# The first layer's output projection beside its last attention head

## The chip, the cores and the metric

The kernel runs on one core of a Trainium2 chip. The metric is device time in microseconds. Its engines have their own instruction queues: TensorE (PE; weight loads stand apart as PEld), VectorE (DVE), ScalarE (ACT), GpSimd (POOL) and SyncE (SP), which only issues transfers here. A profile has the times of one execution.

## The reference, cut to what matters

A two-layer transformer on 1024 image tokens and 256 context tokens, width 1024, in fp32. Layer 0 mixes by differential attention, layer 1 by windowed attention; each is followed by a residual, a norm, and a mixture of 32 experts. What the change touches is the end of layer 0's mixer:

```python
def _diff_attend(q, k, v, lam):
    s = jnp.einsum('bqhmd,bkhmd->bhmqk', q, k).astype(jnp.float32) / math.sqrt(q.shape[-1])
    p = jax.nn.softmax(s, axis=-1)
    a = p[:, :, 0] - lam * p[:, :, 1]
    return jnp.einsum('bhqk,bkhd->bqhd', a.astype(v.dtype), v)
...
    def out_proj(o):
        o = _rmsnorm(o, subln_g) * (1.0 - lam_init)
        return o.reshape(o.shape[0], o.shape[1], -1) @ w_o
    y = out_proj(_sweep_queries(lambda qb: _diff_attend(qb, k_all, v_all, lam), q))
    if not need_ctx:
        return y, None
    qc = qc.reshape(b, -1, DA_HEADS, 2, HEAD_DIM)
    return y, out_proj(_diff_attend(qc, kc, vc, lam))
...
        x = x + g1 * y
        h2 = _modulate(_rmsnorm(x, norm2_g[i]), sh2, sc2).reshape(b * s, d)
```

There are 8 heads of 128 columns, each with two score maps. An image token sees all 1280 keys; a context token only the 256 context keys. The norm in `out_proj` is per head, over 128 columns, with a weight vector of 128 that all heads share.

## The kernel before

Tokens go in ten tiles of 128: 0 to 7 are image, 8 and 9 context. Products of fp32 values run as three matmuls, of a high and a low half on each side (`woh`, `wol`; "hi" is a rounded copy made on ScalarE, "lo" the difference). Outside the experts, a planner sorts each engine's instructions by the priority of their order in the program and by costs of its own, and gives tiles their buffers; a tile waits until the buffer's last reader is done.

`attention0` goes through heads 0 to 7. In head h, for query tile j, it runs a plan, a string of steps written by hand (`PLAN0`, for the last head `PLAN0L`): `S` computes one map's scores into the only score buffer (three PSUM banks), `E` evicts them on VectorE with the row's bound (L590), `X` takes the exponential on ScalarE (L598), `C` combines the two maps (L612 to L615). `T` transposes two key tiles for a pair of query tiles, with copies on ScalarE and VectorE (L543 to L547); `V` multiplies with the values (L556 to L558). `Q` pulls matmuls of the next head's projection (L341), `P` and `K` take its results, `M` advances the modulation vectors (`gen_mods`, on ScalarE and GpSimd), `W` advances a list of weight loads and splits. In head 7 there is no next head: `W` there loads and splits the output projection's weights, `wo_open`, through two raw buffers (L716 on ScalarE, L717 on GpSimd). Each pair's result goes to memory (`o_s`).

Then `oproj` runs the output projection tile by tile, in the order of `PLANO[0]`: `I` loads a tile of `o_s` and of x, `N` norms the heads two tiles ahead (`norm_o`: L771 on ScalarE, L773 and L778 on VectorE, L779 on GpSimd), `A` transposes one tile ahead, `Q` pulls the 48 matmuls of the tile (L805), and for the tile before, `C` adds the residual (L837 to L839), `L` computes the router's logits, `S` and `H` norm (L857), `D` and `E` route. `get_rows` loads four rows of modulation vectors, once for the image tiles and once for the context tiles. `ring_load` prefetches expert weights, seven chunks of 1 MB, two at a step. Layer 1 uses the same function, and there its first three steps run beside the last units of attention.

Of the kernel before, what the change touches and what calls it, by code (L numbers as in the profile page):

```python
# [3 lines left out]

# [37 lines left out]
MODS = (28, 0)  # L42
# [22 lines left out]
PLAN0L = "S0 E0 X0 V P W S1 V T W V V V E1 X1 K C"  # L65
# [29 lines left out]
class Kernel:  # L95
# [8 lines left out]
    def consts(self, es):  # L104
# [27 lines left out]
        self.cos = c.tile([P, NX, 64], F32, name="cos")  # L132
        self.sin = c.tile([P, NX, 64], F32, name="sin")
# [17 lines left out]
        self.gneg = c.tile([P, P], F32, name="gneg")  # L151
# [219 lines left out]


    def attention0(self, es_wo, es_raw):
        nc, tc, A = self.nc, self.tc, self.A
        with ExitStack() as es:
            ea, ep = ExitStack(), ExitStack()
# [3 lines left out]
            ps_t = self.pool(es, "a0t", bufs=2, space=PSUM)  # L380
# [47 lines left out]
            nc.sync.dma_start(self.cos, A["cos"])  # L428
            nc.sync.dma_start(self.sin, A["sin"])
# [5 lines left out]
            nc.vector.tensor_scalar(self.gneg, sg, -(1.0 - LAM0), None, op0=OP.mult)  # L435
# [9 lines left out]
            def new_k(h):  # L445
                K[h] = pk.tile([P, 2, NT * P], F32R, name=f"K{h % 2}")

            def new_v(h):
                V[h] = [pk.tile([P, NT, P], F32R, name=f"V{x}{h % 2}") for x in "hl"]
# [70 lines left out]
            pl = self.pool(es, "a0s", side="right")  # L520
            pS = self.pool(es, "a0S", space=PSUM)
            ps_o = self.pool(es, "a0o", space=PSUM)
            ps_q = self.pool(es, "a0r", bufs=2, space=PSUM)
# [4 lines left out]
            modq = deque([self.gen_mods(blocks[:MODS[0]], pl, ps_t)])  # L528
            self.mods_left = blocks[MODS[0]:]

            trq, mmq = deque(), deque()

            def av(h, j0, a0, a1, ks):
# [5 lines left out]
                def tr(i0):  # L539
# [4 lines left out]
                    at = pl.tile([P, 2, 512], F32R, name="aT", bufs=3)  # L544
# [5 lines left out]
                def mm(i0, at):  # L550
# [8 lines left out]
                    if i0 == n - 2:  # L559
                        st["ot"] = pl.tile([P, 256], F32, name="ot", bufs=2)  # L560
                        nc.scalar.activation(st["ot"], oT, AF.Copy)

                def fin():
# [3 lines left out]
                    ob = pl.tile([P, 2, P], F32, name="ob", bufs=2)  # L567
# [52 lines left out]
            for h in range(8):  # L620
# [13 lines left out]
                for j in range(NT):  # L634
                    n = NT * P if j < NX else 256
                    qk = deque()
                    if nxt:
                        ps = ps_q.tile([P, 512], F32, name="qkv")
                        qk.append(self.gen_qkv_mm(ps, hTl.pop(j), W[h + 1], 0, 384))
                    x = {}  # L640

                    def run(o):
# [23 lines left out]
                        elif o == "W" and parts:  # L666
                            parts.popleft()()

                    for o in (PLAN0 if h < 7 else PLAN0L).split():
                        run(o)  # L670
                    E1 = x["1"][0]
# [9 lines left out]
                    if j % 2:  # L681
# [3 lines left out]
            while modq:  # L685
                pull(modq)
            while trq:
                pull_tr()
            while parts:
                parts.popleft()()  # L690
# [8 lines left out]
    def wo_open(self, l, es, es_raw, bufs=2):  # L699
# [21 lines left out]
    def oproj_open(self, l, es, side, ps_t, ps_y, ytag):  # L721

        nc, tc, A = self.nc, self.tc, self.A
        T = NT if l == 0 else NX
        xsrc = A["xin"] if l == 0 else self.xs[1]
# [33 lines left out]
        def stage_load(t):  # L759
            ot = pl.tile([P, D], F32, name="o_in", bufs=OB[l][0])  # L760
            nc.sync.dma_start(ot, self.os[t * P:(t + 1) * P, :])
            xt = pl.tile([P, D], F32, name="x_in", bufs=OB[l][1])
            self.o["load"] = nc.sync.dma_start(xt, xsrc[t * P:(t + 1) * P, :])
            st[t] = dict(o=ot, x=xt)

        def norm_o(t):
# [3 lines left out]
            sq = pl.tile([P, D], F32, name="sq", bufs=1)  # L770
            nc.scalar.activation(sq, ot, AF.Square)  # L771
# [1024 lines left out]
```

## Time and profile before

| what | value |
|---|---|
| median of 3 runs | 3031.5 us (3025.55 to 3036.97) |
| the profiled execution's own time | 3026.7 us |
| its span, first to last instruction | 3024.9 us |
| mean granted TensorE clock | 0.963 |
| PE, PEld busy | 2798.5, 2365.9 us |
| DVE, ACT, POOL busy | 2366.1, 2100.2, 940.2 us |

Busy times are sums over instructions on an engine; on PE, instructions overlap in a pipeline. The granted clock is a share of 2.4 GHz. The output projection of layer 0 lies between 897 and 1085 us, its last head between 818 and 897.

### The profile page before, as it was taken

The numbers are of one execution on the slowest core, as the hardware profiler recorded it, in microseconds if no ns is written. First come the engines' busy times: TensorE is split into PE (matmuls) and PEld (weight loads), VectorE is DVE, ScalarE is ACT, GpSimd is POOL, SyncE is SP. The second block draws the span as 40 slices with busy tenths as digits, with TensorE's granted clock in tenths as the row PEclk, the third lists the DMA queues.
The fourth block names the chain that finished last, engine by engine and source line by source line (L and its number), as shares of the span: only waits on it lengthen the run. The fifth ranks groups of instructions, "written<-read, shape, count | busy, mean of one in ns | idle before, by whom it ended". The sixth has DMA issues, their size and how long they took to land. (4 is left out here: it accounts for less than half of the span.)

```text
span 3024.9 us, 44265 instructions
## 1 busy us (share of the span) xinstructions
PE 2798.5 (93%) x15262; PEld 2365.9 (78%) x15262; DVE 2366.1 (78%) x4074; ACT 2100.2 (69%) x3725; POOL 940.2 (31%) x857
## 2 busy tenths in 40 slices
PE   7999999999979979999999489998999799999995
PEld 3888888888857768888888478887888688888882
DVE  5778777777778879998999777765666799998996
ACT  5777777777762258888888478876553478888882
POOL 5656665665521111111110344655100111111100
PEclk9999999999989989999999689999999899999997
DMA  7644554444335379999999745434226699999995
GB/s 266 237 160 160 178 177 163 165 162 159 128 104 201 139 276 372 384 379 375 376 374 364 267 163 197 145 141 173 95 100 207 246 365 377 372 369 365 368 384 225
DMA packets 303213, 745.51 MB, mean 246 GB/s; under 512 B 24612, under 2 KB 80520, under 8 KB 287624
## 3 DMA queue, kind: packets, MB, share of 16 engines
q1 hardware_dynamic: 263880, 676.53, 62.2%
q0 software_dynamic: 19584, 41.98, 3.6%
q10 hardware_dynamic: 19520, 24.12, 2.2%
q8 instruction: 122, 2.00, 0.3%
q14 instruction: 107, 0.88, 0.1%
HBM read 680.60 MB, written 91.29 MB: 255 GB/s over the span
## 5 line engine op out<-in xcount | busy, mean ns | idle before, releaser
L1096 DVE TENSOR_TENSOR elo<-wr,ehi 128x1024 fp32r<-128x1024 f32 x768 | 893.5, 1217 | 104.3 <-ACT ehi L1094 104.2
L1094 ACT ACTIVATE ehi<-wr 128x1024 fp32r<-128x1024 f32 x768 | 763.0, 1062 | 3.1 <-DMA wr<-in_wd 1.3
L341 PE MATMUL qkv<-w_hi,hT 128*128 128x384 f32 (+1 forms) x1920 | 546.1, 353 | 14.8 <-ACT hT L312 4.7
L341 PEld LDWEIGHTS qkv<-w_hi,hT 128*128 128x128 f32 x1920 | 355.6, 197 | 31.4 <-issue 14.0
L1123 POOL DMA_INDIRECT y_s<-yb,dI x64 | 65.7, 1026 | 966.5 <-ACT yb L1172 936.9
L341 PE MATMUL qkv<-w_lo,hT 128*128 128x384 f32 (+1 forms) x960 | 336.0, 350 | 0.4 <-POOL w_lo L332 0.4
L1162 PE MATMUL y<-ehi,hidT 128*128 128x512 f32 x1024 | 316.5, 390 | 2.4 <-ACT yb L1172 2.4
L1148 PE MATMUL pg<-ehi,xT 128*128 128x512 f32 x1024 | 291.4, 407 | 3.3 <-ACT ehi L1094 3.3
L1148 PE MATMUL pu<-ehi,xT 128*128 128x512 f32 x1024 | 281.5, 396 | 0.0
L590 DVE TENSOR_SCALAR_CACHE_REDUCE E<-S 128x1280 f32<-128x1280 f32 (+1 forms) x160 | 203.4, 1271 | 61.1 <-PE S L607 59.7
L1162 PEld LDWEIGHTS y<-ehi,hidT 128*128 128x128 f32 x1024 | 191.8, 188 | 43.7 <-ACT yb L1172 3.2
L598 ACT ACTIVATE E<-E,mx 128x1280 f32<-128x1280 f32 (+1 forms) x160 | 191.0, 1194 | 49.6 <-DVE E L590 48.8
L1148 PEld LDWEIGHTS pu<-ehi,xT 128*128 128x128 f32 x1024 | 188.1, 188 | 36.8
L1148 PEld LDWEIGHTS pg<-ehi,xT 128*128 128x128 f32 x1024 | 184.9, 191 | 36.9 <-ACT ehi L1094 4.1
L1162 PE MATMUL y<-elo,hidT 128*128 128x512 f32 x512 | 199.7, 390 | 0.0
L341 PEld LDWEIGHTS qkv<-w_lo,hT 128*128 128x128 f32 x960 | 188.9, 197 | 6.6 <-issue 4.3
L224 ACT ACTIVATE mpr<-mraw,sf 128x256 f32<-128x256 f32 x320 | 145.5, 504 | 28.8 <-POOL macc L227 22.1
L605 PE MATMUL S<-K,Qh 128*128 128x512 f32 (+1 forms) x416 | 152.6, 367 | 13.2 <-DVE E L590 13.1
L1148 PE MATMUL pg<-elo,xT 128*128 128x512 f32 x512 | 160.0, 394 | 0.0
L1148 PE MATMUL pu<-elo,xT 128*128 128x512 f32 x512 | 158.3, 390 | 0.0
L365 POOL TENSOR_TENSOR rd<-rp_a,rp_u 128x256 f32<-128x256 f32 (+1 forms) x96 | 90.7, 945 | 205.4 <-DVE rp_u L360 114.0
L1172 ACT ACTIVATE yb<-y 128x512 f32<-128x512 f32 x126 | 68.5, 595 | 123.7 <-PE y L1162 123.7
(304 smaller groups left out, 6590.0 us busy)
## 6 DMA issues: line engine op xcount, KB each, us to landing
wr<-in_wg SPq DMA_DIRECT2D x128, 1024.0 KB
wr<-in_wu SPq DMA_DIRECT2D x128, 1024.0 KB
wr<-in_wd SPq DMA_DIRECT2D x128, 1024.0 KB
hT<-hTs SPq DMA_DIRECT2D x100, 1024.0 KB
mraw<-in_mod_w SPq DMA_DIRECT2D x80, 512.0 KB
hTs<-hT SPq DMA_DIRECT2D x20, 1024.0 KB
c_y<-y_s SPq DMA_DIRECT2D x28, 512.0 KB
w_raw<-in_a_qkv SPq DMA_DIRECT2D x32, 384.0 KB
```

The source lines that it names most:

```text
L224: nc.scalar.activation(pr[v][:, q], raw[:, q], AF.Copy, scale=self.sf[:, 4 * i + q, v:v + 1])
L341: self.nc.tensor.matmul(ps[:, 0:n], hT[:, a, k, :], W[b][:, k, c0:c0 + n], start=(i == 0), stop=(i == 3 * KC - 1))
L365: nc.gpsimd.tensor_tensor(rd[:, :, 0, :], av, uu, op=OP.add)
L590: nc.vector.tensor_scalar(E[:, 0:n], Sf[:, 0:n], -0.125, None, op0=OP.mult, op1=OP.min, accum_out=mx)
L598: nc.scalar.activation(E[:, 0:n], E[:, 0:n], AF.Exp, bias=mx, scale=-1.0, accum_out=acc)
L605: nc.tensor.matmul(Sf[:, n0:n0 + w], Qh[:, m, j * P:(j + 1) * P], K[h][:, m, o:o + w], start=True, stop=False)
L1094: nc.scalar.activation(hi, raw, AF.Copy)
L1096: nc.vector.tensor_tensor(lo[:, 0:c], raw[:, 0:c], hi[:, 0:c].bitcast(F32), op=OP.subtract)
L1123: nc.gpsimd.indirect_dma_start(out=self.ybs[l], out_offset=bass.IndirectOffsetOnAxis(ap=idx, axis=0), in_=yb, in_offset=None, bounds_check ...
L1148: nc.tensor.matmul(o, xt[:, a, k, :], w[:, q * 512:(q + 1) * 512], start=(k == 0 and a == 0 and w is hi), stop=(k == KC - 1 and w is lo))
L1162: nc.tensor.matmul(y[:, half, :], hT[:, a, k, :], w[:, f], start=(k == 0 and a == 0 and w is hi), stop=(k == 3 and w is lo))
L1172: nc.scalar.activation(yb[:, f], y[:, half, :], AF.Copy)
```

## The change

The projection's steps for the first five tiles are put into the plan of the last head's last five query tiles. For that, the last head takes its tiles in the order 8, 9, 0, ..., 7, and so does the projection. Before the last head, the modulation and the open weighted sums are drained and the pool `a0d` (`pm`) is closed; the eight raw weight tiles are all loaded at its start and split under the second to fourth of its ten tiles. The norm of the heads goes to ScalarE: eight squares with sums and eight scaled copies per tile. The norm's weights, now one column per partition, multiply the rows of the projection's weights at their split; the low half of that split moves from GpSimd to VectorE. Tables for the rotation move to pools of their stages and are loaded again in layer 1. Some buffers move to the pool `pm`, which heads 0 to 6 use.

```diff
-MODS = (28, 0)
+MODS = 28
-PLAN0L = "S0 E0 X0 V P W S1 V T W V V V E1 X1 K C"
+PLAN0L = ("S0 E0 X0 V S1 T W V T E1 X1 W V T V W T V T C",
+          "S0 Q4 E0 X0 T N Q4 T V N S1 Q6 T V N E1 X1 Q4 N T V N Q6 T N V Q8 N T V N Q8 C N Q8 N N")
+ORDER0 = [8, 9] + list(range(8))
+OST0 = 5
...
+    def load_rope(self, pool):
+        self.cos = pool.tile([P, NX, 64], F32, name="cos")
+        self.sin = pool.tile([P, NX, 64], F32, name="sin")
+        self.nc.sync.dma_start(self.cos, self.A["cos"])
+        self.nc.sync.dma_start(self.sin, self.A["sin"])
...
-            nc.vector.tensor_scalar(self.gneg, sg, -(1.0 - LAM0), None, op0=OP.mult)
+            sgT = ps_t.tile([P, 4, P], F32, name="tr")
+            nc.tensor.transpose(sgT[:, 0, :], sg, self.ident)
+            nc.vector.tensor_scalar(self.gneg, sgT[:, 0, 0:1], -(1.0 - LAM0), None, op0=OP.mult)
...
-                K[h] = pk.tile([P, 2, NT * P], F32R, name=f"K{h % 2}")
+                K[h] = (pa, pk)[h % 2].tile([P, 2, NT * P], F32R, name=f"K{h % 2}")
...
-                    at = pl.tile([P, 2, 512], F32R, name="aT", bufs=3)
+                    p = pm if h < 7 and next(nat) % 3 == 2 else pl
+                    at = p.tile([P, 2, 512], F32R, name="aT", bufs=1 if p is pm else 2)
...
-                        st["ot"] = pl.tile([P, 256], F32, name="ot", bufs=2)
+                        st["ot"] = pl.tile([P, 256], F32, name="ot", bufs=1)
...
-                E = pl.tile([P, NT * P], F32, name=f"E{m}", bufs=(4 if m else 2))
+
+                p = pm if m and h < 7 and j % 4 == 3 else pl
+                E = p.tile([P, NT * P], F32, name=f"E{m}", bufs=1 if p is pm else 3 if m else 2)
...
+                    while modq:
+                        pull(modq)
+                    while trq:
+                        pull_tr()
+                    em.close()
                     ea.close()
-                    parts.extend(self.wo_open(0, es_wo, es_raw))
+                    parts.extend(self.wo_open(0, es_wo, es_raw, KC))
+                    for _ in range(KC):
+                        parts.popleft()()
...
-                for j in range(NT):
+                for u, j in enumerate(range(NT) if nxt else ORDER0):
                     n = NT * P if j < NX else 256
+                    ticks = deque()
+                    if not nxt and u == OST0 - 1:
+                        while parts:
+                            parts.popleft()()
+                        es_raw.close()
+                        self.oproj_open(0, es_o, "left", ps_t, ps_q, "qkv")
+                        self.o["start"]()
...
+                    elif u >= OST0:
+                        qk.append(self.o["stage_b"](u - OST0))
+                        ticks.append(self.o["step"](u - OST0, False))
...
+                        elif o == "N":
+                            pull(ticks)
+                        elif o == "W" and parts and (nxt or u):
...
+                    pull(qk, 100)
+                    pull(ticks, 100)
+                    if not nxt and u % 2 == 0:
+                        while trq:
+                            pull_tr()
...
-            nc.scalar.activation(hi[:, k, :], r, AF.Copy)
-            nc.gpsimd.tensor_tensor(lo[:, k, :], r, hi[:, k, :].bitcast(F32), op=OP.subtract)
+            h = hi[:, k, :].bitcast(F32)
+            if l == 0:
+
+                nc.scalar.activation(hi[:, k, :], r, AF.Copy, scale=self.gneg)
+                nc.vector.scalar_tensor_tensor(lo[:, k, :], r, self.gneg, h, op0=OP.mult, op1=OP.subtract)
+            else:
+                nc.scalar.activation(hi[:, k, :], r, AF.Copy)
+                nc.gpsimd.tensor_tensor(lo[:, k, :], r, h, op=OP.subtract)
...
+        tok = (lambda t: ORDER0[t]) if l == 0 else lambda t: t
...
-            sq = pl.tile([P, D], F32, name="sq", bufs=1)
-            nc.scalar.activation(sq, ot, AF.Square)
             w = pl.tile([P, 2, KC], F32, name="ssq", bufs=2)
-            nc.vector.tensor_reduce(w[:, 0, :], sq.rearrange("p (h d) -> p h d", d=P), axis=AX.X, op=OP.add)
-            nc.vector.scalar_tensor_tensor(w[:, 1, :], self.sums[:, t, :], EPS, self.sums[:, t, :],
+            for h in range(KC):
+                sq = pl.tile([P, P], F32, name="sq", bufs=1)
+                nc.scalar.activation(sq, ot[:, h * P:(h + 1) * P], AF.Square, accum_out=w[:, 0, h:h + 1])
+            nc.vector.scalar_tensor_tensor(w[:, 1, :], self.sums[:, tok(t), :], EPS, self.sums[:, tok(t), :],
                                            op0=OP.mult, op1=OP.mult)
             r = self.rsqrt(w[:, 0, :], 1.0 / P, pl, add=w[:, 1, :])
-            ov = ot.rearrange("p (h d) -> p h d", d=P)
-            nc.vector.tensor_tensor(ov, ov, bc(r, P, 2), op=OP.mult)
-            nc.gpsimd.tensor_tensor(ov, ov, bc(self.gneg, KC, 1), op=OP.mult)
+            for h in range(KC):
+                f = slice(h * P, (h + 1) * P)
+                nc.scalar.activation(ot[:, f], ot[:, f], AF.Copy, scale=r[:, h:h + 1])
...
-        if l == 0:
-            ps_t = self.pool(es, f"o{l}t", bufs=2, space=PSUM)
-            ps_y = self.pool(es, f"o{l}y", bufs=2, space=PSUM)
-            es_raw.close()
-            self.oproj_open(l, es, "left", ps_t, ps_y, "y")
...
-            self.o["start"]()
-            t0 = 0
-        else:
-            t0 = 4 * NX + 3 - OSTART
+        t0 = NT - OST0 if l == 0 else 4 * NX + 3 - OSTART
...
             ld = {t: self.combine_load(0, t, pre, 2) for t in order[:3]}
+            self.load_rope(pk)
```

## Rows read from the trace of the kernel before

**Rows 1.** Busy time by stretches of the last head and the projections.

```profile
core 0: us, PE busy (x) PEld busy (x) DVE busy (x) ACT busy (x) POOL busy (x), PEclk, DMA share, GB/s
818.00:861.10 43.10, 31.86 (x147) 24.98 (x147) 30.20 (x45) 28.70 (x45) 20.88 (x8) 0.80 0.33 104
861.10:881.30 20.20, 18.13 (x116) 14.68 (x115) 18.88 (x29) 13.03 (x23) 0.00 (x0) 1.00 0.10 33
881.30:907.40 26.10, 13.84 (x90) 11.30 (x90) 17.26 (x47) 12.94 (x28) 2.34 (x1) 0.79 0.57 186
907.40:1073.00 165.60, 157.63 (x851) 132.00 (x851) 135.29 (x395) 45.52 (x95) 21.48 (x9) 0.98 0.46 162
```

**Rows 2.** Busy time by stretches, layer 1: projection beside attention, then alone.

```profile
2240.00:2275.00 35.00, 35.00 (x218) 29.86 (x217) 24.57 (x68) 23.08 (x45) 0.00 (x0) 1.00 0.26 98
2300.00:2360.00 60.00, 60.00 (x332) 51.13 (x331) 40.50 (x146) 13.72 (x30) 0.00 (x0) 1.00 0.64 224
```

**Rows 3.** Timeline of VectorE, layer 1's projection alone, L857: start, duration.

```profile
2308.83 1.28 DVE L857 SCALAR_TENSOR_TENSOR h<-tmp,rsq,b 128x1024 f32<-128x1024 f32 x1
2323.93 1.28 DVE L857 SCALAR_TENSOR_TENSOR h<-tmp,rsq,b 128x1024 f32<-128x1024 f32 x1
```

**Rows 4.** Groups by line, 897 to 1096: busy, mean ns, idle before.

```profile
L779 POOL TENSOR_TENSOR o_in<-o_in,gneg 128x1024 f32<-128x1024 f32 x10 | 23.8, 2382 | 156.3 <-DVE o_in L778 77.8 <-DVE slot L897 31.4 <-ACT rsq L272 18.3
...
L778 DVE TENSOR_TENSOR o_in<-o_in,rsq 128x1024 f32<-128x1024 f32 x10 | 12.2, 1222 | 0.3
L773 DVE TENSOR_REDUCE ssq<-sq 128x8 f32<-128x1024 f32 x10 | 12.1, 1212 | 3.7 <-ACT sq L771 3.7
...
L870 DVE TENSOR_SCALAR gl<-lgp,m 128x4 f32<-128x4 f32 x10 | 9.3, 934 | 0.0
```

**Rows 5.** Timeline of TensorE, first tiles of the last head.

```profile
818.00 0.39 PE L605 MATMUL S<-K,Qh 128*128 128x512 f32 x1
818.23 0.40 PE L607 MATMUL S<-K,Ql 128*128 128x512 f32 x1
...
821.22 0.39 PE L605 MATMUL S<-K,Qh 128*128 128x256 f32 x1
...
829.98 0.63 PE L607 MATMUL S<-K,Ql 128*128 128x512 f32 x1
830.40 0.63 PE L605 MATMUL S<-K,Qh 128*128 128x512 f32 x1
```

**Rows 6.** Timeline of VectorE, the last key tile of the last head.

```profile
820.73 0.43 DVE L476 TENSOR_TENSOR K<-tr,K 64x256 fp32r<-64x256 f32 x1
```

**Rows 7.** Timeline of VectorE, first and last of the context tiles' four evictions (L590).

```profile
881.31 0.42 DVE L590 TENSOR_SCALAR_CACHE_REDUCE E<-S 128x256 f32<-128x256 f32 x1
...
885.85 0.42 DVE L590 TENSOR_SCALAR_CACHE_REDUCE E<-S 128x256 f32<-128x256 f32 x1
```

**Rows 8.** Groups by line, 818 to 897: the splits of the projection's weights.

```profile
L717 POOL TENSOR_TENSOR wol<-wo_raw,woh 128x1024 fp32r<-128x1024 f32 x8 | 20.9, 2616 | 15.3 <-ACT woh L716 15.3
...
L716 ACT ACTIVATE woh<-wo_raw 128x1024 fp32r<-128x1024 f32 x8 | 8.4, 1054 | 6.3 <-DMA wo_raw<-in_a_wo 6.2
```

**Rows 9.** Timeline of ScalarE, narrow activations at the end of head 6.

```profile
809.21 0.29 ACT L463 ACTIVATE Vh<-qkv 128x128 fp32r<-128x128 f32 x1
...
809.77 0.92 ACT L224 ACTIVATE mraw<-mraw,sf 128x256 f32<-128x256 f32 x2
```

**Rows 10.** Timeline of ScalarE, a table load in layer 1's overlapped part.

```profile
2241.70 0.60 ACT L1532 ACTIVATE aT<-tr 128x512 fp32r<-128x512 f32 x1 [0.42 <-PE tr L1529]
2242.31 1.28 ACT L268 ACT_TABLE_LOAD   x1
2243.61 0.29 ACT L268 ACTIVATE rsq<-ss,eps 128x1 f32<-128x1 f32 x1
```

**Rows 11.** Busy time by stretches, start of layer 1's attention.

```profile
1700.00:1720.00 20.00, 14.45 (x65) 13.37 (x65) 18.72 (x32) 12.19 (x28) 12.68 (x8) 0.59 0.92 325
```

**Rows 12.** Busy time by stretches, in the last head's second tile.

```profile
830.00:835.00 5.00, 3.83 (x12) 2.85 (x11) 2.80 (x3) 4.72 (x6) 3.55 (x2) 0.50 0.44 120
```

More of the change, by code (lines that the diff above doesn't have):

```diff
@@ L3 @@
 from contextlib import ExitStack
+from itertools import count
 import numpy as np
@@ L150, in consts @@
         self.lam = c.tile([P, 1], F32, name="lam")
-        self.gneg = c.tile([P, P], F32, name="gneg")
+        self.gneg = c.tile([P, 1], F32, name="gneg")
         self.dI = c.tile([P, NE], I32, name="dI")
@@ L445, in new_k @@
             def new_k(h):
-                K[h] = pk.tile([P, 2, NT * P], F32R, name=f"K{h % 2}")
+                K[h] = (pa, pk)[h % 2].tile([P, 2, NT * P], F32R, name=f"K{h % 2}")
             def new_v(h):
-                V[h] = [pk.tile([P, NT, P], F32R, name=f"V{x}{h % 2}") for x in "hl"]
+                V[h] = [(pa, pk)[h % 2].tile([P, NT, P], F32R, name=f"V{x}{h % 2}") for x in "hl"]
             new_v(1)
@@ L520, in attention0 @@
             pl = self.pool(es, "a0s", side="right")
+            pm = self.pool(em, "a0d", side="right")
+            ps_q = self.pool(es_o, "a0r", bufs=2, space=PSUM)
             pS = self.pool(es, "a0S", space=PSUM)
             ps_o = self.pool(es, "a0o", space=PSUM)
-            ps_q = self.pool(es, "a0r", bufs=2, space=PSUM)
             S = pS.tile([P, 3, 512], F32, name="S")
@@ L527, in attention0 @@
             blocks = [(0, b) for b in range(8, 24)] + [(1, b) for b in range(24)]
-            modq = deque([self.gen_mods(blocks[:MODS[0]], pl, ps_t)])
-            self.mods_left = blocks[MODS[0]:]
+            modq = deque([self.gen_mods(blocks[:MODS], pm, ps_t)])
+            self.mods_left = blocks[MODS:]
             trq, mmq = deque(), deque()
+            nat = count()
             def av(h, j0, a0, a1, ks):
@@ L566, in fin @@
                         nc.tensor.transpose(pt[:, i, :], st["ot"][:, i * P:(i + 1) * P], self.ident)
-                    ob = pl.tile([P, 2, P], F32, name="ob", bufs=2)
+                    ob = pl.tile([P, 2, P], F32, name="ob", bufs=1)
                     nc.scalar.activation(ob, pt[:, 0:2, :], AF.Copy)
@@ L665, in run @@
                             pull(modq)
-                        elif o == "W" and parts:
+                        elif o == "N":
+                            pull(ticks)
+                        elif o == "W" and parts and (nxt or u):
                             parts.popleft()()
-                    for o in (PLAN0 if h < 7 else PLAN0L).split():
+                    for o in (PLAN0 if nxt else PLAN0L[u >= OST0]).split():
                         run(o)
+                    pull(qk, 100)
[3 more added lines that the diff above has]
+                            pull_tr()
                     E1 = x["1"][0]
@@ L760, in stage_load @@
             ot = pl.tile([P, D], F32, name="o_in", bufs=OB[l][0])
-            nc.sync.dma_start(ot, self.os[t * P:(t + 1) * P, :])
+            ts = slice(tok(t) * P, (tok(t) + 1) * P)
+            nc.sync.dma_start(ot, self.os[ts, :])
             xt = pl.tile([P, D], F32, name="x_in", bufs=OB[l][1])
-            self.o["load"] = nc.sync.dma_start(xt, xsrc[t * P:(t + 1) * P, :])
+            self.o["load"] = nc.sync.dma_start(xt, xsrc[ts, :])
             st[t] = dict(o=ot, x=xt)
@@ L889, in stage_d @@
             nc.vector.tensor_tensor(pr, Aoh, bc(rk[:, 0, 0:NE], 2, 1), op=OP.mult)
-            nc.vector.tensor_reduce(self.r_all[:, t, :], pr, axis=AX.X, op=OP.add)
-            oh = pl.tile([P, 2, P], F32R, name="oh", bufs=2)
-            nc.vector.tensor_tensor(oh, bc(self.iota, 2, 1), bc(self.r_all[:, t, :], P, 2), op=OP.is_equal)
+            nc.vector.tensor_reduce(self.r_all[:, tok(t), :], pr, axis=AX.X, op=OP.add)
+            oh = pl.tile([P, 2, P], F32R, name="oh", bufs=1 + l)
+            nc.vector.tensor_tensor(oh, bc(self.iota, 2, 1), bc(self.r_all[:, tok(t), :], P, 2), op=OP.is_equal)
             vv = pl.tile([P, 2, NE], F32R, name="vv", bufs=2)
-            nc.vector.tensor_tensor(vv, Aoh, bc(self.destp[:, t, :], NE, 2), op=OP.mult)
+            nc.vector.tensor_tensor(vv, Aoh, bc(self.destp[:, tok(t), :], NE, 2), op=OP.mult)
             for a in range(2):
@@ L1710, in build @@
             self.consts(es)
-            ew, eraw = ExitStack(), ExitStack()
-            self.attention0(ew, eraw)
+            ew, eraw, eo = ExitStack(), ExitStack(), ExitStack()
+            self.attention0(ew, eraw, eo)
             if stop == "qkv0":
```

39 lines of the change are left out of this document (15 added, 24 removed).

## The prediction

> **What bounds the kernel now.** I read the page first for the shares, then the busy time by stretches over the last head and the output projection, then the order of instructions in them, and last the groups of instructions by line. The page's shares are means over stages with other limits, so only the stretches decide. In [rows 1] the reader is to see four of them. From 818.0 to 861.1 the last head's first five tiles run with TensorE busy for 31.9 of 43.1 us at a granted clock of 0.80. From 861.1 to 881.3 three undisturbed tiles pass, with VectorE busy for 18.9 of 20.2 us: with no projection of a next head beside it, this stage hangs on VectorE. From 881.3 to 907.4 the two context tiles, the last weighted sums and the first normed tile leave TensorE busy for 13.8 of 26.1 us. From 907.4 to 1073.0 ten output projections take 165.6 us, 16.6 us each; behind them the router ends and the experts begin. So 89 us of attention with about half of TensorE's time unused are followed by 166 us that are mostly TensorE's.
>
> What a projected tile needs when VectorE and GpSimd are out of the way is seen in the second layer, where the same function runs beside attention for three units and then alone: in the part alone TensorE is busy 60.00 of 60 us [rows 2], and one tile follows the other after 15.1 us [rows 3]. In the overlapped part TensorE is also busy for 35.00 of 35 us, with ScalarE at 23.1 [rows 2]. The first layer's tile costs 1.5 us more. Its norm has a 1.22 us multiplication and a 1.21 us sum on VectorE, and a 2.38 us multiplication on GpSimd; and a VectorE instruction of 4 elements takes 0.93 us in the mean [rows 4], since some of them stand until GpSimd's instruction is done.
>
> **The change part by part.** I keep the time axis of the profile before and look for the new place of the last projection matmul, 1073.0 before; what follows it is not touched.
>
> *The start of the last head.* Before, it began at 818.0 with tile 0, whose first 1024 columns need no late key tile; only the last 256 columns waited, until 821.2 [rows 5], for the key tile 9, finished at 820.73 + 0.43 [rows 6]. The new order begins with the context tiles, which need exactly that key tile. So the head starts at 821.2: a loss of 3.2 us that nothing covers. The drains of the previous head's weighted sums and of the modulation lie in the same gap: no further price; at worst 2 us.
>
> *Two context tiles.* Their four evictions stand from 881.31 to 885.85 [rows 7], 4.5 us, and one more such step of 1.1 opens the way to the next tile: 826.8.
>
> *Three tiles without cover.* Three undisturbed tiles took the 20.2 us of the second stretch, 6.7 each [rows 1]. Into the same three slots come the eight weight splits. On ScalarE they stay at 1.05 us each [rows 8]. The low halves move from GpSimd, at 2.62 us each there [rows 8], to VectorE, the engine that binds here; an instruction of that form and size took 1.28 us [rows 3], so 8 × 1.28 = 10.2 us. Bounds: 0, if they fill the gaps of the context tiles, and 14, if the first projection's small VectorE work is caught behind them. I take 10.2, since VectorE has only 1.3 of 20.2 us free. Loading through eight buffers removes the waits in which ScalarE stood on the weight transfers, 6.3 us before [rows 8]; these waits delayed exponentials, and the slots that they filled are not in my 6.7. Projection starts at 826.8 + 20.2 + 10.2 = 857.2. The opening work (two input tiles, their norms, five more transfers) was worth most of 896.9 to 907.4; it is now under tile 2. If that cover fails, the first projection comes some 8 us later.
>
> *Five units of attention with a projection.* TensorE: an attention tile is at most 18.13/3 = 6.0 us [rows 1], a projected one 15.1 [rows 3]: 21.1. VectorE: 18.88/3 = 6.3 and, from the second layer, 40.50/4 = 10.1 [rows 1, 2], with seven short norm instructions of about 0.17: 17.6. ScalarE: 13.03/3 = 4.3, and 13.72/4 = 3.4 [rows 1, 2]; the norm is now sixteen 128-wide activations. One of 128 took 0.29, two of 256 with a scale column took 0.92 together [rows 9]: bounds 4.6 and 7.4 us for sixteen, and I take 5.0, near the 128-wide row. The plan's order puts a square root (of the previous tile's norm) between the two exponentials and another (of the heads' norm) behind them: between two and four table loads a unit. A load and its root begin 1.30 us apart [rows 10]; four are 5.2. ScalarE then has 4.3 + 3.4 + 5.0 + 5.2 = 17.9 us, 85% of TensorE's 21.1.
>
> The Trainium skill prices such a switch higher: "ScalarE: Activation LUTs", section "What ACT_TABLE_LOAD costs", gives about 1283 ns for the load and about 1380 ns for a drain, 2.66 us, and its rule is to group functions by table set, which this order does not. The load's 1.28 us agrees with the row; of the drain that row shows nothing, as the load begins right where the activation before it ends. By the page's figure four switches would be 10.6 us and ScalarE 23.3, above TensorE (an estimate).
>
> So TensorE sets the pace, with three engines at 85, 83 and nearly 100%. Some instructions will wait in order: between 0 and 4 us a unit, and I take 1.5: 5 × 22.6 = 113.0. The weighted sums of tile 2 also fall here, some 3 us of TensorE. That ends at 857.2 + 113.0 + 3 = 973.2.
>
> *Five projections alone,* at 15.1: the two big VectorE instructions and the GpSimd one are gone, and with them the difference to the second layer. 75.5 us: 1048.7. The second set of rows for the residual is now loaded in an overlapped unit, under attention. The ring of expert weights loads its seven chunks later, under these 75 us; over the projections before, transfers were at 0.46 with the same chunks among them [rows 1], so I price it at nothing; without that cover the experts would start late by what is still on its way.
>
> *Elsewhere.* The tables for the rotation are loaded a second time, 0.5 MB, in a stretch with transfers at 0.92 and 325 GB/s [rows 11]: 1.5 us, between 0 and 3. The transposition of the norm's weights falls where TensorE is idle: 0, at most 1. Buffers in other pools keep their counts in heads 0 to 6: 0.
>
> *Sum:* 1048.7 − 1073.0 + 1.5 = −23 us. Against the profiled execution's own 3026.7 us that is 3003.7; its time is 4.8 below the median of the runs, 3031.5, so for the median I give 3008.5.
>
> **The rivals.**
>
> *ScalarE becomes the bound.* For it: four table switches a unit, and ScalarE is in order, so a norm that waits for its input holds the exponentials behind it. Against it: the second layer's overlapped part kept TensorE at 35.00 of 35 with ScalarE at 66% [rows 2]. If ScalarE needs 25 us a unit (7.4 for the norm, 2 us of standing), five units take 125 instead of 113: gain 11, 3020.5. The skill's page would give about the same place: 23.3 us and some waiting a unit.
>
> *The overlap does not come about.* The engines' order is made by a planner from its own costs. If the first projections wait for the normed tile or for the row transfers, and go behind the attention, the stages stand in line as before, and only 10 × 1.5 us of the shorter projection is left, against 3.2 at the start and 10.2 of splits: 3030, no change.
>
> *TensorE's clock falls in the overlapped units* and the kernel is slower. At the clock of 0.5 (1.2 of 2.4 GHz) two 512-wide matmuls start 0.42 us apart, at 1.0 0.23 [rows 5]; it was granted 0.50 in a stretch where TensorE, in the waits on the eviction of scores, was busy 3.8 of 5 us [rows 12]. If waits on ScalarE split the matmuls likewise, the 21.1 us become 39, five units 90 us more: 3100 in full. It decides from 4.6 us a unit on (23 over five), that is, once a quarter of each unit runs at the lower level; at a half, 3031.5 − 23 + 45 = 3053.5. Against it: in 861.1 to 881.3, with TensorE busy 90%, the clock was 1.00 [rows 1].
>
> **How the numbers follow.** Forecast as worked out: 0.70, and its own range 2994 to 3019: 40 us of gain if the splits and waits cost nothing, 12 with both at their upper ends. ScalarE as the bound 0.13, no overlap 0.09, the clock 0.08. The range 2990 to 3026 takes in the first two cases and leaves the last out, with part of the third. A measurement of this kernel can tell about 0.5%, 15 us, from no change. Faster by more, below 3016: nearly all of the first case and a third of the second: 0.71. Within 0.5%: 0.20. Slower: 0.09.
>
> **What would show it.** In the profile after: the first scores of the last head are those of a 256-wide tile near 821; the low halves of the weights stand on VectorE, near 1.3 us each; the first projection matmul lies near 857, with score matmuls behind it; tiles then follow after 22 to 23 us and, alone, after 15.1; the last projection matmul ends near 1049; GpSimd is idle there; table loads in the overlapped units are between 10 and 20. The prediction is wrong if the units take over 25 us with ScalarE busy throughout, if the granted clock drops in them, or if the three tiles before take over 40 us.

## The result, and the profile after

| kernel | median, us | range, runs | ratio to before, interval |
|---|---|---|---|
| before | 3031.5 | 3025.55 to 3037.1, 5 | |
| changed, first set | 3010.11 | 3005.78 to 3018.98, 5 | 0.9945, 0.993 to 0.996 |
| changed, second set | 3016.24 | 3005.63 to 3017.97, 6 | 0.9943, 0.9927 to 0.996 |

The change is worth 0.55%, with the forecast of 3008.5 near the first median. All eleven runs have a median of 3015.9 and leave a gap: five lie between 3005.6 and 3010.5, six between 3015.9 and 3019.0. The profiled execution is the slowest of them, 3018.98 us (span 3016.9), 8 us under that of before; the median hides how far single steps were off. A second profile, of a run of 3010.52 us, comes with experiment 6.

Busy time by stretches of the changed kernel, from its last head's first full tile to the last projection matmul, answers to [rows 1]:

```profile
core 0: us, PE busy (x) PEld busy (x) DVE busy (x) ACT busy (x) POOL busy (x), PEclk, DMA share, GB/s
835.00:855.00 20.00, 11.19 (x35) 8.43 (x36) 19.80 (x27) 15.23 (x19) 0.00 (x0) 0.64 0.54 199
855.00:868.40 13.40, 8.71 (x24) 5.86 (x23) 7.57 (x19) 13.06 (x42) 0.00 (x0) 0.50 0.62 247
...
868.48:891.30 22.82, 22.78 (x134) 19.48 (x135) 12.14 (x24) 14.60 (x34) 0.00 (x0) 0.94 0.03 7
891.30:911.00 19.70, 19.70 (x116) 16.96 (x115) 14.12 (x38) 15.31 (x43) 0.00 (x0) 1.00 0.38 134
911.00:941.10 30.10, 27.85 (x163) 22.45 (x161) 22.18 (x69) 26.27 (x73) 0.00 (x0) 1.00 0.47 163
941.10:961.10 20.00, 20.00 (x118) 17.30 (x118) 14.03 (x43) 13.91 (x38) 0.00 (x0) 0.91 0.22 79
961.10:981.40 20.30, 20.28 (x119) 17.21 (x118) 15.93 (x43) 16.96 (x41) 0.00 (x0) 1.00 0.37 137
981.40:1002.60 21.20, 21.20 (x137) 18.34 (x136) 15.55 (x58) 16.60 (x53) 0.00 (x0) 1.00 0.50 173
1002.60:1062.60 60.00, 60.00 (x332) 50.67 (x331) 43.68 (x169) 24.60 (x80) 0.00 (x0) 1.00 0.60 204
```

VectorE sets the first stretch (19.80 of 20 us). In the second nothing but ScalarE is full, while TensorE waits for the first normed tile. From 868.5 each row is about one projected tile, the last one four of them, and TensorE is full in nearly all. GpSimd is idle.

The timeline of TensorE of the same kernel shows the two places that the sum did not have, the prologue and the opening of the projections (idle time ahead of an instruction, and its releaser, in brackets):

```profile
38.18 0.33 PE L443 MATMUL tr<-ident,sg 128*128 128x128 f32 x1
42.08 1.11 PE L304 MATMUL tr<-ident,n_xn 128*128 128x128 f32 x4 [3.58 <-DVE rsq L271]
43.79 1.12 PE L304 MATMUL tr<-ident,n_xn 128*128 128x128 f32 x4 [0.59 <-DVE gneg L444]
46.37 1.12 PE L304 MATMUL tr<-ident,n_xn 128*128 128x128 f32 x4 [1.46 <-DVE n_hf L312]
48.42 1.12 PE L304 MATMUL tr<-ident,n_xn 128*128 128x128 f32 x4 [0.94 <-ACT n_hf L310]
51.80 0.69 PE L343 MATMUL qkv<-w_hi,hT 128*128 128x384 f32 x1 [2.27 <-ACT hT L314]
...
857.85 0.79 PE L619 MATMUL S<-K,Qh 128*128 128x512 f32 x1 [1.59 <-DVE E L604]
...
865.95 2.53 PE L832 MATMUL tr<-ident,o_in 128*128 128x128 f32 x8 [1.51 <-ACT o_in L821]
868.48 0.80 PE L847 MATMUL qkv<-woh,oT 128*128 128x512 f32 x1
```

The second half of the first normed input waits for `gneg`: the transposed weights (L443) hold one of the two "tr" buffers. The wait itself is 0.59 us; the halves of the inputs behind it then go one by one, each behind a copy of a half before it (1.46 and 0.94 us). Head 0's first projection matmul comes at 51.80; before, it was at 44.73. The first eviction of scores follows at 120.20, against 114.32, and at the end of head 6 the kernel is 6.4 us late. The second profile has 118.0 for the first eviction and is about 3 us late there.

Groups of the changed kernel by line, VectorE from 826 to 870 and ScalarE from 868 to 1003, answer to [rows 3, 8, 9, 10]:

```profile
L604 DVE TENSOR_SCALAR_CACHE_REDUCE E<-S 128x1280 f32<-128x1280 f32 x7 | 10.4, 1486 | 3.4 <-PE S L621 3.4
L754 DVE SCALAR_TENSOR_TENSOR wol<-wo_raw,gneg,woh 128x1024 fp32r<-128x1024 f32 x8 | 9.9, 1279 | 0.0
...
L821 ACT ACTIVATE o_in<-o_in,rsq 128x128 f32<-128x128 f32 x56 | 17.7, 391 | 1.9 <-DVE rsq L282 1.9
L815 ACT ACTIVATE sq<-o_in 128x128 f32<-128x128 f32 x52 | 15.9, 306 | 2.1 <-DMA o_in<-o_s 1.2
...
L815 ACT ACTIVATION_READ_ACCUMULATOR sq<-o_in 128x1 f32 x52 | 9.8, 189 | 0.0
L612 ACT ACT_TABLE_LOAD x7 | 9.0, 1283 | 0.1
...
L274 ACT ACT_TABLE_LOAD x6 | 7.7, 1283 | 0.2
...
L270 ACT ACT_TABLE_LOAD x2 | 2.6, 1283 | 0.0
```

Fifteen table loads, and low halves at 1.279 us each, as forecast.

### The profile page after: what moved, and what is told of

Read it like the earlier page. It is cut to its first block, busy times and chain, and to the rows that moved or that the text cites. A ratio compares the mean times of both kernels' runs of the same rounds, so it can differ in the third digit from the quotient of the medians.

```text
span 3016.9 us, 44424 instructions
## 1 busy us (share of the span) xinstructions
PE 2801.4 (93%) x15263; PEld 2367.6 (78%) x15263; DVE 2328.5 (77%) x4062; ACT 2162.8 (72%) x3969; POOL 898.7 (30%) x839
## 5 line engine op out<-in xcount | busy, mean ns | idle before, releaser
L847 PE MATMUL qkv<-woh,oT 128*128 128x512 f32 x576 | 203.4, 413 | 0.1
```

Source lines behind the costliest of these rows:

```text
L847: nc.tensor.matmul(y, oT[:, a, k, :], w[:, k, half * 512:half * 512 + 512], start=(i == 0), stop=(i == 3 * KC - 1))
```

## The experiments

**1. The weights' column without TensorE.**

```diff
-            sgT = ps_t.tile([P, 4, P], F32, name="tr")
-            nc.tensor.transpose(sgT[:, 0, :], sg, self.ident)
+            sg = pre.tile([P, 1], F32, name="sg")
+            nc.sync.dma_start(sg, A["a_subln"].rearrange("(p o) -> p o", o=1))
```

> The changed kernel with the norm's weights brought into a column by their DMA, so that TensorE's transposition of them and its PSUM buffer are gone from the prologue. Theory: that transposition holds one of the two buffers in which the first layer's normed inputs are transposed, and cost the prologue 5.9 us (first eviction of scores at 120.20 us, 114.32 before the change). Then the first eviction comes back to 114 to 115, the experts start 5 to 6 us earlier than 1085.9, and the median falls by some 6 us from 3010. Rival: the prologue is longer because of the other order of loads and pools: first eviction still near 120, no change of the time.

First eviction at 115.1: 5.1 us are back, and the timeline of TensorE has the form of before again:

```profile
42.19 1.90 PE L304 MATMUL tr<-ident,n_xn 128*128 128x128 f32 x8 [3.85 <-DVE rsq L271]
45.49 0.69 PE L343 MATMUL qkv<-w_hi,hT 128*128 128x384 f32 x1 [1.40 <-ACT hT L314]
```

So the cause holds for the prologue. The time does not follow: 3015.24 (3011.31 to 3017.93), against 3015.9 over the changed kernel's eleven runs, and the experts start at 1086.4. The lead is gone before the last head, whose first eviction stands at 828.5, against 828.6 and 824.9 in the changed kernel's two profiles. A first part goes in head 0, where TensorE waits longer for ScalarE's `ot`, as it did before (3.76 us); this kernel's line, then the changed one's:

```profile
147.93 0.54 PE L576 MATMUL tr<-ident,ot 128*128 128x128 f32 x2 [3.72 <-ACT ot L571]
```

```profile
152.57 0.44 PE L578 MATMUL tr<-ident,ot 128*128 128x128 f32 x2 [1.68 <-ACT ot L573]
```

In head 3 the profile loses 2 us, where TensorE stood 2.45 us on an input tile (1.69 in the changed kernel) and its granted clock was 0.67 in the 5 us behind; in head 4 the rest goes too.

**2. The kernel before, with the transposition and the second load of the tables.**

```diff
+            sgT = ps_t.tile([P, 4, P], F32, name="tr")
+            nc.tensor.transpose(sgT[:, 0, :], sg, self.ident)
+            gcol = pre.tile([P, 1], F32, name="gcol")
+            nc.vector.tensor_scalar(gcol, sgT[:, 0, 0:1], -(1.0 - LAM0), None, op0=OP.mult)
...
+            nc.sync.dma_start(self.cos, self.A["cos"])
+            nc.sync.dma_start(self.sin, self.A["sin"])
```

> The kernel before with two things of the change alone: the transposition of the norm's weights in the prologue (its result goes unused), and the second load of the rotation's tables ahead of the second layer's attention. Theory: first eviction of scores at 120 instead of 114.3, all of head 0 to 7 later by 5 to 6 us; the second load costs 0 to 3 us between the last expert of the first layer and the second layer's first scores; time 5 to 9 us above the kernel before, some 3038. Rival: both are hidden, 3031.

First eviction 117.7, 3.4 us late, less than the theory's 5 to 6. With the transposition the first eviction lies between 117.7 and 120.7 in all profiles, without it between 114.3 and 115.1: it costs the prologue 3 to 6 us with either kernel around it. The 3.4 us are still 3.4 when the experts start and 3.5 at layer 1's first projection, so the second load of the tables costs nothing in this profile. The median is 3033.61, not the theory's 3038, with a ratio of 1.0009 (0.9995 to 1.0024): a loss of this size hardly shows in whole times.

**3. No overlap.**

```diff
-OST0 = 5
+OST0 = 10
```

> The changed kernel with the number of attention tiles ahead of the first projection set to all ten: context tiles first, norm on ScalarE, folded weights and eight load buffers stay, but no projection runs beside attention. Theory (the prediction's): the overlap is where the gain comes from; without it only ten times 1.5 us of the shorter projection is left against the splits and the late start: 3025 to 3032, some 20 us above the changed kernel. Rival, from the trace of the changed kernel: TensorE is nearly full in both orders, an attention tile without cover takes 6.7 us and a projection alone 15.1, 21.8 against the 23.6 that an overlapped unit took; the last projection matmul then lies between 1050 and 1064 (1062.5 in the changed kernel) and the time is within 12 us of the changed kernel's, more likely below.

3024.97 (3016.63 to 3031.08), and the last projection matmul at 1070.2. From the last head's first eviction that is 244.7 us, against 233.9 and 232.9 in two profiles of the changed kernel: 11 us, about half of what the theory gave, and more than the rival's last matmul at 1064 allowed; the median is 9 us above that of the changed kernel's eleven runs. Its timeline of TensorE shows one wait, and the stretches show what came behind it:

```profile
957.95 1.94 PE L860 MATMUL tr<-ident,b 128*128 128x128 f32 x8 [4.66 <-DMA b<-mod_s]
```

```profile
953.00:958.00 5.00, 0.34 (x3) 0.09 (x2) 0.00 (x0) 0.00 (x0) 0.00 (x0) 0.81 1.03 389
958.00:963.00 5.00, 5.00 (x24) 4.76 (x24) 2.52 (x3) 1.48 (x4) 0.00 (x0) 0.50 0.32 129
963.00:968.00 5.00, 5.00 (x19) 4.06 (x19) 2.83 (x7) 3.25 (x13) 0.00 (x0) 0.66 0.26 105
```

TensorE stands on the second set of rows, whose buffers come free only when the second tile is done, and then runs at 0.50.

**4. No overlap, and no second set of rows.** Experiment 3 with

```diff
-            v = 0 if tok(t) < NX else 1
+            v = 0
...
-            get_rows(0 if tok(0) < NX else 1)
+            get_rows(0)
```

> The kernel without overlap again (all ten attention tiles ahead of the first projection), and with one set of rows for the residual and the second norm for all ten tiles, so that the second set is not loaded: the context tiles' results are computed with the other tiles' rows. The experts then get other tokens, so it is read up to the last projection matmul of the first layer, from the last head's first eviction. That stretch was 244.7 us without overlap (825.5 to 1070.2), 233.9 and 232.9 in the two profiles of the changed kernel. Theory: what the overlap buys is cover for the second set of rows, on which TensorE stood for 4.66 us without it, with a granted clock of 0.50 for 10.2 us behind it; without that load the stretch is 234 to 237 us. Rival: running the projections beside attention is worth its 11 us by itself: 242 to 245.

826.4 to 1058.2 is 231.8 us, less than with the overlap; the left-out set saves some 2 us of TensorE itself (an estimate: 1.06 us for such a transposition at a granted clock of 1.00, and about as much for the eight small matmuls behind it). The rival falls: beside a projection that keeps TensorE full, attention wins nothing; what the overlap buys is cover for that one load.

The kernel before had no such wait to cover. It comes to the context tiles last, and the transposition of its second set stands between projections without idle time ahead of it:

```profile
1054.89 0.40 PE L805 MATMUL y<-woh,oT 128*128 128x512 f32 x1
1055.13 1.03 PE L818 MATMUL tr<-ident,b 128*128 128x128 f32 x8
```

The change takes the context tiles first, and so needs the second set after two tiles: the wait that the overlap covers is one that the new order brings.

**5. Two load buffers.**

```diff
-                    parts.extend(self.wo_open(0, es_wo, es_raw, KC))
-                    for _ in range(KC):
+                    parts.extend(self.wo_open(0, es_wo, es_raw, 2))
+                    for _ in range(2):
```

> The changed kernel with two buffers for the projection's weights instead of eight: the loads are again issued in pairs, each behind the splits of the pair before. Theory: ScalarE stands on these loads as it did before (6.3 us in all), the last splits end later than 852, and the first projection matmul comes 3 to 8 us later than 868.5; time 3 to 8 us above the changed kernel. Rival: the opening of the projections is bound by the attention tiles at the lower granted clock, and the first projection matmul stays within 2 us of 868.5.

First projection matmul at 876.0, of which 1.4 us are a later start of the head: 6.1 us, as the theory has it. The last projection matmul comes 238.5 us behind the head's first eviction, against 233.9 and 232.9, so some 5 us remain. The time does not show them: 3016.48 (3010.52 to 3017.86), against 3015.9.

**6. The changed kernel again.** 

> The changed kernel again, beside the three others of this set. Every theory: median 3010, within the 3005.8 to 3019.0 of its first runs; first projection matmul near 868.5, experts' start near 1086. It shows how far one profile of a kernel lies from another.

3016.24. First projection at 864.3 with a head that began 3.7 us earlier. The end of the profiled span is 8.5 us earlier; half of that arises at one place, the opening of layer 1's projections. TensorE's wait there in the changed kernel's two profiles, first and second:

```profile
2211.16 1.07 PE L860 MATMUL tr<-ident,b 128*128 128x128 f32 x8 [2.18 <-DMA b<-mod_s]
```

```profile
2207.05 1.06 PE L860 MATMUL tr<-ident,b 128*128 128x128 f32 x8 [1.14 <-DMA b<-mod_s]
```

and the stretches that follow:

```profile
2213.00:2218.00 5.00, 5.00 (x24) 4.72 (x24) 1.48 (x3) 2.27 (x6) 0.00 (x0) 0.50 0.00 0
2218.00:2223.00 5.00, 5.00 (x25) 4.05 (x25) 3.10 (x8) 1.56 (x4) 0.00 (x0) 0.83 0.00 0
```

```profile
2209.00:2214.00 5.00, 5.00 (x34) 4.33 (x34) 3.16 (x6) 2.73 (x9) 0.00 (x0) 1.00 0.00 0
```

Between 2202 and 2232 the first profile loses 4.2 us of its lead over before.

**7. The opening cut in two.** The call of `start` ahead of the fifth attention tile is left with the loads and the first norm; the rest of it comes behind that tile:

```diff
-                        self.o["start"]()
+                        self.o["start"](0)
...
+                    if not nxt and u == OST0 - 1:
+                        self.o["start"](1)
```

> The changed kernel with the opening of the projections cut in two: its loads and the first norm stay ahead of the fifth attention tile, and the transposition of the normed tile, the rows for the residual and the second norm come behind that tile, so that the weighted sums of tiles 0 and 1, which take the same two PSUM buffers, run first. Theory: in the changed kernel these sums stand behind the opening's transpositions in buffer order, and TensorE has nothing to do but scores from 853 to 866 at a granted clock of 0.50; moved up, some 7 us of transpositions and sums leave the stretch 875 to 888, the clock rises earlier, and the last projection matmul falls from 1062.5 to 1055 to 1059; time 3 to 7 us less. Rival: the sums only delay the normed tile, the first projection comes as much later as is won behind it: no change within 2 us, or up to 5 us more.

3008.18 (3002.68 to 3012.96). The weighted sums now run from 856, and TensorE is busy for 15.63 of the 19.8 us up to the first projection at 874.9. That is 47.3 us behind the last head's first eviction, against 39.8 in the changed kernel; but the last projection matmul comes 230.9 us behind it (1058.5), against 233.9 and 232.9: 2 to 3 us won, just under the lower end of the theory (3.5 to 7.5). The ratio to before, 0.9924 (0.9908 to 0.9939), is not clear of the changed kernel's.

**8. The roots on VectorE.** A shift, a subtraction and three Newton steps for `AF.Sqrt` in `norm_o` and `stage_s`:

```diff
+        nc.vector.tensor_scalar(ri, v.bitcast(I32), 1, None, op0=OP.logical_shift_right)
+        nc.vector.tensor_scalar(ri, ri, -1, 0x5f3759df, op0=OP.mult, op1=OP.add)
...
-            r = self.rsqrt(w[:, 0, :], 1.0 / P, pl, add=w[:, 1, :])
+            r = self.rsqrt_v(w[:, 0, :], 1.0 / P, pl, add=w[:, 1, :])
```

> The changed kernel with the first layer's roots (of the heads' norm and of the second norm in the projections) taken on VectorE, by a shifted integer and three Newton steps, instead of by the square root of ScalarE: some 17 table loads of 1.28 us, 21.8 us, leave ScalarE in the overlapped units, and VectorE has six more instructions of about 0.17 us per root. Theory: TensorE paces the units and ScalarE has room, so the units keep their length (19.6, 30.2, 19.9, 20.3, 21.1 us between projected tiles); only the opening, where two table loads stand ahead of the first normed tile, wins 1 to 3 us. Rival: ScalarE is the pace of the units, and they win up to 21.8 us in all. Second rival: the longer chain of small VectorE instructions delays the normed tile, 0 to 5 us more.

No table load is left in the units, and ScalarE's busy time over them falls from 103.65 us of 134.1 to 83.00 of 134.6:

```profile
867.20:891.00 23.80, 23.75 (x133) 20.24 (x134) 12.85 (x20) 11.68 (x29) 0.00 (x0) 0.91 0.14 51
891.00:1001.80 110.80, 107.41 (x647) 91.31 (x646) 92.17 (x341) 71.33 (x215) 0.00 (x0) 1.00 0.39 132
```

Nothing else changes: the first projection stands at 867.2 with a head 1.1 us earlier, and the time is 3013.45 (3012.09 to 3021.27). ScalarE is not the pace; nor did the opening win its 1 to 3 us.

**9. Filled waits.**

```diff
+                            if not nxt and 1 < u < OST0:
+                                fill = ps_q.tile([P, 512], F32, name="qkv")
+                                for i in range(5):
+                                    nc.tensor.matmul(fill, Qh[:, 0, 0:P], K[h][:, 0, 0:512], start=(i == 0), stop=(i == 4))
```

> The changed kernel with five more 512-wide matmuls behind each of the six score blocks of the three uncovered tiles, into a buffer that nobody reads: they fill TensorE's waits on the eviction and compute nothing that is used. Theory: the granted clock of 0.50 from 841 to 872 comes from these waits and costs 0.7 us per score map (4.09 us from eviction to eviction, against 3.37 before the change at 1.00); filled, the clock stays at 1.00 longer, and the first projection matmul comes 3 to 5 us earlier, and so does all behind it. Rival: the maps hang on VectorE with its eight low halves of weights, or on the added matmuls: first projection within 1 us of 868.5, or later.

3018.22, first projection at 867.9. It tests little of the theory: the added matmuls depend on nothing, so they all ran by 838.5, and from 842 TensorE waits as before. The clock stayed at 1.00 from 840 to 845 (0.57 in the changed kernel), and the first projection still comes 39.5 us behind the head's first eviction, against 39.8. The evictions at 834.0, 838.4 and 842.3 stand 4.4 and 3.9 us apart at a granted clock of 1.00, with VectorE at 5.00 of 5 us: there it is VectorE, not the clock.

**10. Half of the low halves on GpSimd.**

```diff
+                if k % 2:
+                    nc.gpsimd.tensor_scalar(r, r, self.gneg, None, op0=OP.mult)
+                    nc.gpsimd.tensor_tensor(lo[:, k, :], r, h, op=OP.subtract)
...
```

> The changed kernel with four of the eight low halves of the folded weights on GpSimd, in two instructions each (product with the norm's weight in place, then the difference), and four left on VectorE. Theory: VectorE, busy for 20 of 20 us from 835 to 855, sets the pace of the three uncovered tiles, and each low half of 1.24 us on it costs its full time; four fewer bring the first projection matmul 3 to 5 us nearer, and the time falls by as much. Rival: GpSimd's pairs are so long, or hold VectorE up so much while they run, that the last low half ends no earlier than the 852 of the changed kernel: first projection as before, or up to 10 us later.

The rival. The first projection stands at 871.5, with a head that began 0.3 us earlier: 3.4 us later. The time is 3014.14 (3012.23 to 3019.16). The timeline of GpSimd, then that of VectorE beside it:

```profile
842.14 4.11 POOL L755 TENSOR_SCALAR wo_raw<-wo_raw,gneg 128x1024 f32<-128x1024 f32 x1
...
852.59 2.79 POOL L756 TENSOR_TENSOR wol<-wo_raw,woh 128x1024 fp32r<-128x1024 f32 x1
855.36 2.84 POOL L755 TENSOR_SCALAR wo_raw<-wo_raw,gneg 128x1024 f32<-128x1024 f32 x1
858.28 2.35 POOL L756 TENSOR_TENSOR wol<-wo_raw,woh 128x1024 fp32r<-128x1024 f32 x1
```

```profile
846.94 2.86 DVE L758 SCALAR_TENSOR_TENSOR wol<-wo_raw,gneg,woh 128x1024 fp32r<-128x1024 f32 x1
...
853.17 2.24 DVE L820 SCALAR_TENSOR_TENSOR ssq<-sums 128x8 f32<-128x8 f32 x1
```

A pair takes 5.3 to 6.7 us on GpSimd, the last ends at 860.6, and VectorE's own low half goes from 1.28 to 2.86, an instruction of 8 elements to 2.24.

**11. The rows ahead of the second tile's inputs**, the second norm's offset (`b2`) first, in both layers.

```diff
             stage_load(0)
-            stage_load(1)
...
             get_rows(0 if tok(0) < NX else 1)
+            stage_load(1)
```

> The changed kernel with the opening's loads in another order, in both layers: the rows for the residual, that of the second norm's offset first, are loaded before the second tile's inputs instead of behind them. Theory: in the second layer TensorE stood on that row, for 2.18 us in the first profile and 1.14 in the second, and the granted clock fell to 0.50 for 6.8 us only in the first, 4.2 us of time: that is what parts the runs near 3017 from those near 3008. With the row loaded earlier the wait is under 1 us, there is no fall at the opening of the second layer's projections in any profile, and the median lies 3 to 6 us below the 3016 of the changed kernel's eleven runs; the runs lie closer together. Rival: the spread comes from elsewhere, and the runs still lie between 3006 and 3019.

3010.03 (3007.03 to 3019.9). TensorE no longer waits for that row in layer 1, and its clock stays up there. Five of six runs lie below 3012, one at 3019.9: the wait is one source of the spread, not all of it. In layer 0 the same edit does not help: the last projection matmul comes 236.9 us behind the last head's first eviction, against 233.9 and 232.9. The ratio to before, 0.9933 (0.9911 to 0.9953), is not clear of the changed kernel's.

**12. Experiments 1, 7 and 11 together.** 

> The changed kernel with three edits together: the weights' column by DMA (no transposition in the prologue), the opening cut in two with the weighted sums ahead of its transpositions, and the rows loaded before the second tile's inputs. Theory: 5 us in the prologue, 2 to 3 in the last head, 0 to 4 in the second layer's opening, of which the clock's falls in between may give some back: 3000 to 3008, at least 8 us under the changed kernel's 3016. Rival: what is won in one place is lost in the next wait: 3008 to 3016.

3001.79 (2998.11 to 3003.56), ratio 0.99 (0.9883 to 0.9917): faster than both kernels, with every run below every run of the changed one. First eviction 114.4, last projection matmul 1054.4 (1062.5), layer 1's 2340.6 (2356.3). The prologue's 5 us are not among the gain: the last head's first eviction stands at 826.7, between the 824.9 and 828.6 of the changed kernel's profiles, as in experiment 1. The gain lies behind it: the last projection matmul comes 227.7 us behind that eviction, and layer 1's projections take 148.8 us from first to last matmul, against 154.6 and 150.2.

## Why the prediction came out, and where it did not

Its steps, forecast on the time axis of before and measured in the changed kernel's first profile:

| step | forecast, us | measured, us |
|---|---|---|
| last head starts | at 821.2 | at 828.12 |
| two context tiles | 5.6 | 4.5 |
| three tiles with the splits | 30.4 | 25.2 |
| opening not covered | 0 | 10.6 |
| five units beside attention | 116 | 112.9 |
| five projections behind them | 75.5 | 81.1 |
| last projection matmul | at 1048.7 | at 1062.5 |

In the second profile the head starts at 824.4, and the first and the last projection matmul stand at 864.3 and 1057.8.

**The transposition, "where TensorE is idle: 0, at most 1".** It failed. TensorE was idle, but the resource was the buffer, one of two, held until VectorE had read it. It cost the prologue 3.4 to 5.9 us. Whether any of that is left in the 6.9 us by which the last head starts late is not shown: without the transposition it starts at 828.0 and 826.1 (experiments 1 and 12), with it at 828.1 and 824.4. What else makes it late stays open.

**The splits, 10.2 us.** Right: 8 × 1.279, VectorE full for 19.80 of 20 us, and half of them on GpSimd was no better (experiment 10). The three tiles around them were charged 20.2 from rows with weighted sums among them; without these they took some 15 (25.2 less 10.2).

**The opening "now under tile 2".** It failed, and the 8 us named for that were 10.6. One input of the first tile is issued at 846.7, behind the store of the context tiles' result; the rest follow from 852.3, when the last low half has freed the raw weights' space. Then come thirteen squares, a root between two table loads, and eight products, while the weighted sums that could have filled TensorE stand behind the opening in the order of the "tr" buffers. Experiment 7 moves them.

**The units.** Right in size and cause: 22.6 us with TensorE at 98%, VectorE at 15.7 and ScalarE at 17.4 us a unit over the five from 868.5 to 981.4, against 22.6, 17.6 and 17.9; the scores of the first unit had run in the opening. The norm was 5.9 us instead of 5.0 (a square with its accumulator starts every 0.44), and three loads, not four, made up for it. The rival of ScalarE as the bound falls by experiment 8. The Trainium skill ("ScalarE: Activation LUTs", "What ACT_TABLE_LOAD costs") gives a drain beside the load; the loads here are 1.283 us, and without fifteen of them the six units took 134.6 us against 134.1 (experiment 8).

**Five projections alone.** Four follow at 15.1; the first takes 21.2, since the last pair's weighted sums run beside it. The 3 us charged for sums were those of tile 2; these were left out.

**What the overlap is for.** The sum drew the gain from TensorE's idle half in the last head. That step failed. Its own terms said so: 22.6 us for an overlapped unit, against 6.7 and 15.1, 21.8, one after the other. Experiments 3 and 4 show that without overlap the idle half shrinks as well, and that the overlap is worth only the wait on the second set of rows, 11 us with the clock behind it. The prediction priced that load at nothing because of the overlap; covering it is all that the overlap does, and the kernel before, with its other order, did not have to. The gain over before is elsewhere. From the last head's first eviction to the last projection matmul it took 251.0 us before, and 231.8 in experiment 4, without overlap and without the second set: 73.8 instead of 85.6 up to the first projection, of which the eight buffers are some 5 (experiment 5) and the rest is not separated, and 158.0 instead of 165.4 behind it, with projections alone at 15.1 instead of 16.6.

**The clock.** It fell, as the rival said, but in the three tiles and the opening (0.50 from 845 to 870) and hardly in the units (0.91 to 1.00); what that alone costs stays open, since experiment 9 did not fill the waits.

That the median came within 2 us is in part luck: by all eleven runs it is 7 us off, by the profiled execution 15, and the gain that the sum took from the overlap came from other steps.

## What to carry to other kernels

An idle engine does not make an instruction free: ask also which buffer it takes, in which order that buffer goes round, and who reads it last. Before overlapping two stages, count whether the full engine would be any shorter; if not, the gain is a covered wait, and moving that one load may do (not tried here). A wait of TensorE costs its length and, in several places here, a lower clock behind it, so loads that TensorE waits for go first in their queue. A gain in one stage has to be followed to the end: the prologue's 5 us were gone five heads later.

## What the runs showed of the hardware

One and the same wait of TensorE, on the row `b` at the opening of layer 1's projections, stands in twelve profiles. The granted clock stayed at 1.00 behind it after 0.77, 1.01, 1.14, 1.15, 1.62, 1.66 and 1.72 us idle (experiments 3, 10, 6, the kernel before, 1, 5 and 7), and was 0.50 or 0.51, from 1.8 to 6.8 us behind the end of the wait, after 1.45, 1.78, 1.90, 2.13 and 2.18 us (experiments 2, 8, 9, 4 and the changed kernel's first profile). So the length of the wait alone does not decide: 1.45 us had the fall, and 1.72 did not. Between the two profiles of the changed kernel the longer wait and the fall are worth 4.2 us together. It does not sort the runs by itself: of the changed kernel and its variants with this load in its old place and with the overlap, those with the fall took 3018.7 to 3020.2 us, those without it 3008.4 to 3017.9.

Beside GpSimd's instructions VectorE's became longer (experiment 10): 128x1024 from 1.28 to 2.86 us, and one of 8 elements from some 0.2 to 2.24.
